# A decoder trunk with power-of-two weight scales: the cross-partition maxima of 20 of 22 scales are turned through DRAM instead of by TensorE

## The chip, the cores and the metric

The program runs on one core of one Trainium2 chip. The metric is the device time of one execution in microseconds (us); the kernel before takes 1691.45 us (median of three runs, 1690.5 to 1695.71). Engines are named as in the profile: PE (TensorE matmul), PEld (its weight load), DVE (VectorE), ACT (ScalarE), POOL (GpSimd), SP (SyncE, which here only issues DMAs).

## What is computed

A residual stream x of 2048 tokens by 1024 goes through one recurrent layer (layer A) and one attention layer (layer B), all in float32. Layer B reads keys and values that are projected once from layer A's output.

```python
def rglru_layer(x, ...):                       # layer A
    u = rmsnorm(x, norm_g) @ w_in              # 1024 -> 2 * 1536
    xb, gate = u[..., :LRU_WIDTH], u[..., LRU_WIDTH:]
    xb = causal_depthwise_conv(xb, conv_w, conv_b)
    r = sigmoid(blockdiag(xb, wr) + br); i = sigmoid(blockdiag(xb, wi) + bi)
    a = exp(-8 * r * softplus(-lam)); b = sqrt(1 - a * a) * (i * xb)
    hs = scan(h[t] = a[t] * h[t - 1] + b[t])
    return x + (hs * silu(gate)) @ w_out
# layer B: rmsnorm, q/gate projection, sliding-window attention
# with sinks and ALiBi, gate, output projection, residual
```

## The kernel before

**Two-part numbers.** Matmuls take f16 operands. Each float32 operand is scaled by a power of two and split into a high and a low f16 part (`split_flat`: ACT makes the high part, DVE the low one), and a product takes three passes. The scale of a weight matrix or of an activation comes from its largest magnitude. DVE finds a maximum per partition; `floor2` (line 95) then makes of `[128, n]` such maxima the largest of each column over all partitions, rounded down to a power of two, on every partition. That is the function that the change replaces.

**floor2 before** takes six steps on two engines. PE transposes the column into PSUM (`f2t`, line 100); DVE reduces the row to one number (`f2m`, 102), bounds it below (`f2n`, 104), masks the mantissa away (`f2o`, 106) and scales a small identity by it (`f2d`, 108); PE multiplies that by ones, which puts the number on all partitions (`f2b`, 110, two passes of the array); DVE copies it out of PSUM (111). Both PE steps stand in PE's queue between products that have nothing to do with them.

**Stages.** (1) The start loads and normalizes the first 512 tokens and the first weights. (2) Layer A runs 16 units: 4 groups `g` of three 128-channel tiles by 4 chunks `c` of 512 tokens. A unit (`unit`, line 370) is 72 products `pu` (x-branch), 72 products `pg` (gate branch) and 36 products `pr` (the two recurrence gates, `gate`, line 407). ACT copies `pu` out of PSUM into `u`; DVE convolves it to `xc`; ACT and POOL (DVE for one of three tiles) split `xc` into `hl`, which `pr` reads; SP copies a third of a block between partitions (`b3<-hl`, line 395), which the last 9 products of each gate read. The PSUM tiles of `pu`, `pg` and `pr` take turns in six banks, so the second gate's tiles wait until DVE has read the `pg` tiles (`gs<-pg`, line 404). Then ACT makes r, i, a and the square root, and DVE runs `ri`, `q`, the scan `h`, and the running maximum `ymx`. (3) The output projection of layer A: 16 token blocks of 72 products `po` (`out_block`, line 591), with `xnT<-xnT,sy` as the split of a block's input, two blocks ahead. (4) Layer B.

**Work beside a unit** comes from generators (`run_side`). While group g runs, the weights of group g + 1 are prepared: `prep_part` (263) loads two halves into `st`, reduces them (`amx`, `mx`, `m`), calls `floor2`, and splits into `w`; `prep_gates` (287) does the same for the gate weights `gst`. In group 0 the side work is the second weight half of group 0 and the normalization of the next chunk (`norm_chunk`, 248), whose result is turned by a DMA transpose (`flip`, 210: `xnT<-xs`). In group 3 it is the scale and split of `w_out` (`w_out_scale`, `w_out_prep`), and `y_scale` (541) turns `ymx` of a chunk into `sy`. Beside stage 3, `prep_rows` and `w_outB_scale` (665) make the weights of layer B.

**What sets the order.** Every engine runs its own queue strictly in order. A list scheduler fills the queues from priorities and its own estimates of durations; `floor2` is issued 200 places ahead (`tc.high_priority(offset=F2AHEAD)`). SP's queue holds all loads, the `b3` copies and the transposes, one after the other: a DMA whose condition is not met holds up all that stand behind it on SP.

**Calls of floor2:** the first weight half of group 0 and `conv_bounds` (both in the start), and 20 more: the other weight halves (`pw`, 4 + 3), the gate weights (`pwg`, 4), `w_out` (`pwo`), four chunks of y (`py`), and four weight sets of layer B (`pw_kv`, `pw_q`, `pw_g`, `pw_o`).

Of the kernel before, what the change touches and what calls it, by code (L numbers as in the profile page):

```python
# [12 lines left out]
F32 = mybir.dt.float32  # L13
# [3 lines left out]
U32 = mybir.dt.uint32  # L17
# [19 lines left out]
PREP_AT = (((1, 0), (3, 1), (7, 2), (9, 3)), ((1, 4), (3, 5), (5, 6), (7, 7)), ())  # L37
# other products woven in (columns / 2.4) after a block's pair of scores, before the first
# and the second half of its values; for the first block, the second, those between, the
# last but one, the last  # L40
GAPS = ((700, 8000, 9500), (300, 8000, 10500), (700, 8000, 9500), (800, 8000, 12000), (900, 11000, 9500))
# [12 lines left out]
def trunk(ctx, tc, x, wA, gw, par, gains, woA, wkv, wB, woB, vec, alib, out):  # L54
# [12 lines left out]

    # ---------------------------------------------------------------- constants
    id16 = xp.tile([P, P], F16, name="id16")
# [18 lines left out]

    cnt = [0]

    def uniq(s):
        cnt[0] += 1
        return f"{s}_{cnt[0]}"

    def floor2(mx, n, keep):
        """[P, n] maxima -> keep [P, n]: each column's maximum over the partitions, rounded
        down to a power of two, on every partition"""
        with tc.high_priority(offset=F2AHEAD):
            tp = pst([n, P], F32, "tp", uniq("f2t"), 2)
            pe.transpose(tp, mx, id32)  # L100
            m1 = xp.tile([n, 1], F32, tag="f2m", name=uniq("f2m"), bufs=2)
            dve.tensor_reduce(m1, tp, AX.X, ALU.max)
            m2 = xp.tile([n, 1], F32, tag="f2n", name=uniq("f2n"), bufs=2)
            dve.tensor_scalar(m2, m1, 1e-30, None, ALU.max)
            m3 = xp.tile([n, 1], F32, tag="f2o", name=uniq("f2o"), bufs=2)
            dve.tensor_scalar(m3.bitcast(U32), m2.bitcast(U32), 0x7F800000, None, ALU.bitwise_and)
            dg = xp.tile([n, n], F32, tag="f2d", name=uniq("f2d"), bufs=2)
            dve.tensor_scalar(dg, id32[:n, :n], m3, None, ALU.mult)
            bp = pst([P, n], F32, "tp", uniq("f2b"), 2)
            pe.matmul(bp, ones[:n, :], dg, start=True, stop=True)  # L110
            dve.tensor_copy(keep, bp)

    def col(name, n=1):
        return tmp[0].tile([P, n], F32, tag=f"{name}{n}", name=uniq(name), bufs=2)
# [3 lines left out]

    # ------------------------------------------------ conv and decay parameters
    cb2 = xp.tile([P, 2], F32, name="cb2")  # L120
# [13 lines left out]
    def decay():  # L134
        # softplus(-lam) = max(-lam, 0) + log1p(exp(-|lam|)), log1p(e) = 2 atanh(e / (2 + e))
        nlam = xp.tile([P, KR], F32, name="nlam")
# [25 lines left out]

    # ------------------------------------------------------------ shared pieces
    def wtile(name):
        return wp.tile([P, 2, 3072], F16, tag="W", name=name, bufs=4)

    def absmax_rows(src, nk, gcol, dest):
        """largest |gain * w| per partition of src [P, nk, n] -> dest [P, 1]"""
        a = col("amx", nk)
        dve.tensor_reduce(a, src, AX.X, ALU.max, apply_absolute_value=True)  # L170
        dve.tensor_tensor(a, a, gabs[:, gcol : gcol + nk], ALU.mult)
        dve.tensor_reduce(dest, a, AX.X, ALU.max)
# [6 lines left out]
    def split_flat(src, scale, hi, lo):  # L179
        """hi + lo = src * scale in two f16 parts"""  # L180
        act.activation(hi, src, AF.Copy, scale=scale)
        dve.scalar_tensor_tensor(lo, src, scale, hi, ALU.mult, ALU.subtract)  # L182

    def rstd10(ss, eng):
        """2**10 / rms of rows of D from their sums of squares"""
        var = col("var")
        eng.tensor_scalar(var, ss, 1.0 / D, EPS, ALU.mult, ALU.add)
        rs = col("rs")
        pool.tensor_tensor(rs, var, mhalf[:, 0:1], ALU.pow)
        r10 = col("r10")  # L190
        eng.tensor_scalar(r10, rs, 1024.0, None, ALU.mult)
        return r10

    def normalize(xb, hi, lo, rs=pool):
        """hi + lo = rows of xb [P tok, D] over their rms, times 2**10"""
        ss = col("ss")
        act.activation(lo.bitcast(BF16), xb, AF.Square, accum_out=ss)
        split_flat(xb, rstd10(ss, rs), hi, lo)
# [11 lines left out]
    def flip(src, dest):  # L210
        """dest[:, i, :] = the transpose of src[:, i * P : (i + 1) * P], two-byte types"""
        nc.sync.dma_start_transpose(dest, src)
# [12 lines left out]

    # ======================================================= layer A, channel-major
    p1pool = ExitStack()
# [16 lines left out]
    def xparts():  # L244
        """two [P, D] f16 tiles"""
        return tuple(p1.tile([P, D], F16, tag=f"ri{w}", name=uniq("xri"), bufs=4) for w in range(2))
# [60 lines left out]
    def scales_x(g, W):  # L307
        # |conv(u) + b| <= sum|w| * 2**11 px + max|b|
        px = W["p0"]
# [42 lines left out]
    def proj_first(w):  # L352
        """the first chunk's three tiles, token block by token block"""
        o = [pst([P, CH], F32, "mm", uniq("pu"), 6) for _ in range(3)]
# [15 lines left out]
    def unit(g, c, W):  # L370
# [36 lines left out]
        def gate(w):  # L407
            gt = W["gt"]
            o = [pst([P, CH], F32, "mm", uniq("pr"), 6) for _ in range(3)]
            for j in range(3):  # L410
                for n, (wi, xi) in enumerate(PASSES):
                    mm(o[j], gt[:, wi, w, j * P : (j + 1) * P], hls[j][:, xi], n == 0, False)
            # the fourth block, gathered, on the array's columns 0, 32 and 64
            for n, (wi, xi) in enumerate(PASSES):
# [60 lines left out]

    # ---- the first weights and tokens
    W0 = {}
# [26 lines left out]
    conv_bounds()  # L504
    scales_x(0, W0)

    def first_side():
# [72 lines left out]

    # ============================================================== out-proj of A
    bw = ctx.enter_context(tc.tile_pool(name="bw", bufs=1, side="right", reuse_waits="tile"))
# [39 lines left out]
    def bstage(n):  # L622
        """[P, n] f32 staging, n <= 2048"""
        stg[0] += 1
# [64 lines left out]
    for b in range(NB):  # L689
# [4 lines left out]
        if b == NB - 3:  # L694
            drain(side)
            # the first block of layer B
            fx = xnT[3].bitcast(F32)[:, 0:D]
# [5 lines left out]

    # ======================================================= layer B, token-major
    psA.close()
# [19 lines left out]

    # keys carry g_q * g_k / 8, scaled by a power of two
    gg = p3.tile([P, HD], F32, name="gg")
# [9 lines left out]
    dve.tensor_scalar(gk, gg, igg, 2048.0, ALU.mult, ALU.mult)  # L737
    # slopes halve from head h to head h + 2: queries of head h carry 2**(4 + h // 2), and
    # two tables do for all heads
    qsc = p3.tile([P, HEADS], F32, name="qsc")  # L740
# [16 lines left out]
    def eps_of(key, name):  # L757
        # eps in the units of the projection: eps * (2**24 / p)**2
        i = p3.tile([P, 1], F32, name=name + "i")
# [10 lines left out]
    dve.tensor_scalar(gscB, pB["g"], 2.0**-24, None, ALU.mult)  # L770
    # out = P * p_y * (p_wo * p_kv * 2**-31): y carries 2**3 / p_kv, its parts 2**14 / p_y, w_out 2**14 / p_wo
    cB = p3.tile([P, 1], F32, name="cB")
# [3 lines left out]
    def proj3(o, xt, w, n0, n1, nk=KD):  # L776
        """o[tok, n0:n1] = x @ w in three passes; yields their length after every few products"""
        i = 0
# [22 lines left out]
    def project(b):  # L801
# [3 lines left out]
        yield from proj3(kv, xt, kvrow, 0, 256)  # L805
        # ---- keys
        kn = p3.tile([P, 2, HD], F32, tag="kn", name=uniq("kn"), bufs=1)
# [22 lines left out]
        d["kT"] = kt  # L830
        # ---- values: |v| * 2**24 / p < 2**35, kept times 2**-21
        v32 = p3.tile([P, 2, HD], F32, tag="v32", name=uniq("v32"), bufs=2)
# [11 lines left out]
        d["v32"], d["vt"] = v32, vt  # L844
        # ---- queries
        qn = p3.tile([P, HEADS, HD], F32, tag="f4", name=uniq("qn"), bufs=2)
# [40 lines left out]
    def attend(b):  # L887
        """yields how much else the PE is to do, as in GAPS"""
        gaps = GAPS[b if b < 2 else max(2, b - NB + 5)]
# [39 lines left out]
        def turn(n, ph):  # L929
            flip(ph.rearrange("p w h n -> p (w h n)"), pT.rearrange("p w h n -> p (w h) n"))  # L930
            for w in range(2):
                # slot j > query q belongs to the block before
                pool.affine_select(  # L933
# [59 lines left out]
    def gated(b, y, i, parts):  # L993
        """part i of y times the gate, in two f16 parts, transposed"""
        d = st[b]
# [34 lines left out]
    def hooked(gen, hooks):  # L1030
        """gen with f run before its i-th item for the pairs i, f of hooks"""
        for i, t in enumerate(gen):
# [5 lines left out]
    def between(b):  # L1038
        """what the PE does beside block b's attention"""
        if b + 3 < NB:  # L1040
# [21 lines left out]
    def weave(main, fill):  # L1062
        """runs main; while it waits, takes as much from fill"""
        debt = 0.0
# [27 lines left out]
def _layout(inputs):  # L1092
# [3 lines left out]
    for g in range(NTRI):  # L1096
        for i, w in enumerate((wr, wi)):
# [5 lines left out]
            o[0:96, 384:480] = b[3]  # L1103
    # channels: tile j of a triple has block j and a third of block 3
    perm = []
# [54 lines left out]
```

## Time and profile before

| | us |
|---|---|
| median of three runs (lowest, highest) | 1691.45 (1690.5, 1695.71) |
| span of the profiled execution | 1695.6 |
| PE busy, share of the span | 1550.7 (91%) |
| DVE busy | 1198.8 (71%) |
| ACT busy | 742.7 (44%) |
| POOL busy | 475.5 (28%) |

The profiled execution's own time is its span, 1695.6 us; what lies around the span is not listed apart, and the slowest of the three runs, 1695.71, is 0.1 above it. A row of the timeline gives start, length, engine, line, operation, tile written <- tiles read, count, and in brackets the idle time of the engine just before, with what ended it. "PEclk" is the share of full clock that was granted to TensorE. A row of the groups gives count, busy time and mean length in ns, then the idle time just before such instructions with what ended it.

### The profile page before, as it was taken

The page shows a single profiled execution, that of the slowest core. Times are in us where ns is not written, and L with a number is a line of the kernel's source. Part 1 is how long each engine was busy: PE and PEld are TensorE (multiplying, and loading weights), DVE is VectorE, ACT ScalarE, POOL GpSimd, SP SyncE. Part 2 cuts the span into 40 slices and gives each one's busy share as a digit, 9 for nine tenths or more (in the row PEclk, how much of TensorE's full clock was granted, in tenths as well). Part 3 has the DMA queues.
Part 4 walks back from the last instruction along what each step waited for, and adds up shares of the span by engine and source line. Part 5 has one row for each costly group of instructions (what it writes and reads, how often), then busy time and mean ns, then how long its engine had stood idle before and what let it go on. Part 6 is the DMA issues. An engine that isn't in the chain of part 4 may idle for free.

```text
span 1695.6 us, 23216 instructions
## 1 busy us (share of the span) xinstructions
PE 1550.7 (91%) x8602; PEld 765.2 (45%) x8602; DVE 1198.8 (71%) x2700; ACT 742.7 (44%) x1229; POOL 475.5 (28%) x578
## 2 busy tenths in 40 slices
PE   5988889999999998999799978899999999999986
PEld 4433334444444443444344434455555555555543
DVE  6768878688766677766521269777777777777775
ACT  5656546555445465422200154434444434444332
POOL 2234222211222323000000233524343334334331
PEclk9999999999999999999899989999999999999999
DMA  6563212014311133677731334353344444444322
GB/s 206 142 135 92 79 54 80 24 54 127 106 36 32 57 109 112 220 246 260 283 98 62 117 92 91 78 103 84 85 91 91 91 91 90 88 91 90 66 63 66
DMA packets 242194, 177.29 MB, mean 105 GB/s; under 512 B 204704, under 2 KB 215200, under 8 KB 242080
## 3 DMA queue, kind: packets, MB, share of 16 engines
q1 hardware_dynamic: 233632, 146.95, 33.7%
q0 software_dynamic: 8304, 28.84, 5.0%
q8 instruction: 67, 1.10, 0.3%
q14 instruction: 47, 0.39, 0.1%
q10 hardware_dynamic: 144, 0.01, 0.0%
HBM read 92.93 MB, written 29.36 MB: 72 GB/s over the span
## 4 chain that ended last, share of the span: by engine, by line
PE 35%; DVE 24%; DMA 13%; issue 13%; POOL 7%; ACT 7%; SPq 0%; POOLq 0%; ACTq 0%; DVEq 0%
PE po L117 9%; PE pg L117 9%; PE pu L117 7%; PE pf L117 5%; DMA ppx<-ph 5%; DVE s L906 3%; PE pr L117 3%; DVE s L967 2%; DVE xc L390 2%; POOL hl L393 2%; DVE s L962 2%; DMA x<-x1D 1%; DVE h L448 1%; POOL ppx L933 1%; DMA st<-in_wA_dram 1%
## 5 line engine op out<-in xcount | busy, mean ns | idle before, releaser
L117 PEld LDWEIGHTS <-w 128*128 128x128 f16 x2520 | 238.8, 100 | 274.5 <-issue 22.2
L117 PE MATMUL pu<-xnT,w 128*128 128x512 f16 (+1 forms) x1368 | 262.2, 353 | 3.9 <-ACT ri L423 3.4
L117 PEld LDWEIGHTS <-xT 128*128 128x128 f16 x1920 | 186.9, 98 | 169.8 <-issue 3.8
L117 PE MATMUL pg<-xnT,w 128*128 128x512 f16 x1152 | 259.2, 386 | 0.2 <-DVE w L182 0.2
L117 PE MATMUL po<-wo,xnT 128*128 128x512 f16 x1152 | 252.7, 382 | 1.2 <-ACT ri L423 1.2
L117 PE MATMUL pf<-wob,yT 128*128 128x512 f16 x768 | 186.0, 395 | 3.0 <-DMA yT<-wob 1.9
L117 PE MATMUL pq<-wq,xT 128*128 128x512 f16 x768 | 175.9, 379 | 2.6 <-DVE gs L884 2.6
L117 PEld LDWEIGHTS <-xnT 128*128 128x128 f16 x1152 | 113.0, 98 | 137.5 <-issue 4.9
L117 PE MATMUL pg<-wq,xT 128*128 128x512 f16 x768 | 174.3, 381 | 0.0
L117 PEld LDWEIGHTS <-yT 128*128 128x128 f16 x768 | 74.7, 101 | 88.0 <-issue 7.1
L117 PE MATMUL po<-vt,ppx 128*128 128x128 f16 (+1 forms) x1024 | 65.8, 222 | 49.0 <-DMA ppx<-ph 33.6
L390 DVE SCALAR_TENSOR_TENSOR xc<-u,cwS,xc 128x512 f32<-128x512 f32 x144 | 109.5, 783 | 0.1
L933 POOL TENSOR_SCALAR_AFFINE_SELECT ppx<-ppx 128x1024 f16<-128x1024 f16 x64 | 79.0, 1256 | 65.7 <-DMA ppx<-ph 65.7
L117 PEld LDWEIGHTS <-ppx 128*128 128x128 f16 x1024 | 57.1, 107 | 79.6 <-DMA ppx<-ph 42.1
L385 POOL COPY uhist<-u 128x3 f32<-128x3 f32 x36 | 22.8, 633 | 235.9 <-ACT u L379 235.8
L117 PE MATMUL s<-kT,qT 128*128 128x256 f16 x512 | 75.2, 275 | 12.8 <-DVE s L962 11.7
L950 DVE TENSOR_TENSOR y<-y,po 128x256 f32<-128x256 f32 x64 | 26.7, 417 | 84.9 <-ACT y L949 84.6
L617 DVE SCALAR_TENSOR_TENSOR xnT<-po,cA,xnT 128x512 f32<-128x512 f32 x32 | 23.8, 747 | 88.4 <-PE po L117 88.4
L423 ACT ACTIVATE ri<-pr,pr,rsc 128x512 f32<-128x512 f32 x96 | 67.5, 776 | 42.4 <-PE pr L117 42.3
L906 DVE TENSOR_SCALAR s<-s,ssc,bi 128x128 f32<-128x128 f32 x256 | 84.4, 400 | 0.6
L393 POOL TENSOR_TENSOR hl<-xc,hl 128x512 f16<-128x512 f32 x32 | 58.7, 1842 | 83.9 <-ACT hl L392 83.8
L392 ACT CAST hl<-xc 128x512 f16<-128x512 f32 x48 | 29.6, 617 | 120.1 <-DVE xc L390 113.4
(239 smaller groups left out, 2358.3 us busy)
## 6 DMA issues: line engine op xcount, KB each, us to landing
xnT<-in_wB_dram SPq DMA_DIRECT2D x16, 1024.0 KB, 6.8
yD<-gs POOLq DMA_DIRECT2D x48, 256.0 KB, 2.8
wst<-in_woA_dram SPq DMA_DIRECT2D x24, 512.0 KB, 4.7
xnT<-yD SPq DMA_DIRECT2D x16, 768.0 KB, 6.3
st<-in_wA_dram SPq DMA_DIRECT2D x15, 768.0 KB, 5.4
xs<-in_x_dram SPq DMA_DIRECT2D x16, 512.0 KB, 5.0
xnT<-in_x_dram SPq DMA_DIRECT2D x16, 512.0 KB, 4.4
x1D<-xnT POOLq DMA_DIRECT2D x16, 512.0 KB, 3.3
```

The source lines that it names most:

```text
L117: pe.matmul(o, lhsT, rhs, start=start, stop=stop, skip_group_check=True)
L385: pool.tensor_copy(uhist[:, t], u[:, CH : CH + 3])
L390: dve.scalar_tensor_tensor(xc, u[:, d : d + CH], cw[:, j, d : d + 1], xc, ALU.mult, ALU.add)
L392: act.copy(hl[:, 0], xc)
L393: (pool if j in LO_POOL else dve).tensor_tensor(hl[:, 1], xc, hl[:, 0], ALU.subtract)
L423: act.activation(v, o[j], AF.Sigmoid, bias=pr[:, t, 5 + w : 6 + w], scale=W["rsc"])
L617: dve.scalar_tensor_tensor(xs_, o[n], cA[c], xs_, ALU.mult, ALU.add)
L906: dve.tensor_scalar(s[:, h], s[:, h], ssc[:, h : h + 1], bi[:, h : h + 1], ALU.mult, ALU.add)
L933: pool.affine_select(pU[:, w], pT[:, w], [[0, 8], [-1, P]], ALU.is_gt, 0.0, base=0, channel_multiplier=1)
L950: dve.tensor_tensor(yv, yv, o[:, :, 0], ALU.add)
L962: dve.copy_predicated(sl, mask.unsqueeze(1).to_broadcast([P, 2, P]), o[:, :, 0:P])
L967: dve.tensor_tensor_reduce(s[:, h], s[:, h], al[:, i * P : (i + 1) * P], 1.0, -3.4e38, ALU.add, ALU.max, mr[:, h : h + 1])
```

## The change

After the start, `floor2` no longer uses PE. The `[128, n]` maxima are written to a DRAM tile `f2r` as rows of 128 numbers (one DMA that writes 4 bytes from each partition); a second DMA reads that row back to all 128 partitions (`f2w`, 512 bytes into each); DVE reduces it (`f2m`), bounds it and masks it, straight into the result. Both DMAs are issued by SP, the second after the first has landed. The first two calls stay as they were.

```diff
+    started = [False]
-    def floor2(mx, n, keep):
+    def floor2_pe(mx, n, keep):
         with tc.high_priority(offset=F2AHEAD):
             tp = pst([n, P], F32, "tp", uniq("f2t"), 2)
             pe.transpose(tp, mx, id32)
...
             pe.matmul(bp, ones[:n, :], dg, start=True, stop=True)
             dve.tensor_copy(keep, bp)
+    def floor2(mx, n, keep):
+        if not started[0]:
+            floor2_pe(mx, n, keep)
+            return
+        with tc.high_priority(offset=F2AHEAD):
+            turned = dr.tile([n, P], F32, name=uniq("f2r"))
+            nc.sync.dma_start(turned.rearrange("n p -> p n"), mx)
+            row = xp.tile([P, n, P], F32, tag="f2w", name=uniq("f2w"), bufs=2)
+            nc.sync.dma_start(row, turned.unsqueeze(0).to_broadcast([P, n, P]))
+            m1 = xp.tile([P, n], F32, tag="f2m1", name=uniq("f2m1"), bufs=2)
+            dve.tensor_reduce(m1, row, AX.X, ALU.max)
+            m2 = xp.tile([P, n], F32, tag="f2m2", name=uniq("f2m2"), bufs=2)
+            dve.tensor_scalar(m2, m1, 1e-30, None, ALU.max)
+            dve.tensor_scalar(keep.bitcast(U32), m2.bitcast(U32), 0x7F800000, None, ALU.bitwise_and)
...
     conv_bounds()
     scales_x(0, W0)
+    started[0] = True
```

The scheduler lays out the queues anew. On PE, the 20 pairs of `f2t` and `f2b` are gone and the products follow each other in the same order. On PE in the output projection, where block 9 begins (`xnT_99` is block 8's input, `xnT_97` that of block 9), the queue before reads:

```order
L117 MATMUL po_6942<-wo_6061,xnT_99 128x512
L117 LDWEIGHTS xnT_97
L117 MATMUL po_7045<-wo_5134,xnT_97 128x512
L100 MATMUL f2t_7004<-id_74,m_7002 1x128
L117 LDWEIGHTS xnT_97
L117 MATMUL po_7045<-wo_5134,xnT_97 128x512
```

`f2t_7004` waits there for `m_7002`, the maximum of layer B's output weights; in the changed queue block 9's products stand without it.

On DVE at the turn from group 0 to group 1 (`m_2099` and, changed, `m_1958` and `m_2083` are the partition maxima of weights; `ri` is work of the unit that ends), before:

```order
L293 TENSOR_REDUCE m_2099<-gst_2097 128x1
L102 TENSOR_REDUCE f2m_1975<-f2t_1973 1x1
L104 TENSOR_SCALAR f2n_1977<-f2m_1975 1x1
L106 TENSOR_SCALAR f2o_1979<-f2n_1977 1x1
L108 TENSOR_SCALAR f2d_1981<-id_74,f2o_1979 1x1
L111 COPY pw_300_1972<-f2b_1983 128x1
L102 TENSOR_REDUCE f2m_2104<-f2t_2102 1x1
```

and changed:

```order
L292 TENSOR_REDUCE m_1958<-mx_1921 128x1
L311 TENSOR_REDUCE m_2083<-gst_2081 128x1
L461 SCALAR_TENSOR_TENSOR ri_1641<-xc_1376,isig_333,ri_1641 128x512
L461 SCALAR_TENSOR_TENSOR ri_1643<-xc_1426,isig_333,ri_1643 128x512
L461 SCALAR_TENSOR_TENSOR ri_1645<-xc_1476,isig_333,ri_1645 128x512
L126 TENSOR_REDUCE f2m_297_1965<-f2w_1963 128x1
L128 TENSOR_SCALAR f2m_298_1967<-f2m_297_1965 128x1
L129 TENSOR_SCALAR pw_294_1960<-f2m_298_1967 128x1
```

The three `ri` now stand between the maxima and the reduction that needs them back from DRAM.

On SP at the end of the first unit (group 0, chunk 0; `st` are weight loads, `b_65` is that unit's `b3`, `xnT_98` the transposes for chunk 1), before:

```order
L261 DMA st_1733<-in_wA_dram 128x4x384
L261 DMA st_1901<-in_wA_dram 128x4x384
L395 DMA b_65_349<-hl_705 32x1024
L239 DMA xs_104<-in_x_dram 128x1024
L395 DMA b_65_349<-hl_650 32x1024
L395 DMA b_65_349<-hl_800 32x1024
L212 DMA_TRANSPOSE xnT_98<-xs_103 128x16x128
L212 DMA_TRANSPOSE xnT_98<-xs_104 128x16x128
```

and changed:

```order
L413 DMA b_65_349<-hl_701 32x1024
L413 DMA b_65_349<-hl_650 32x1024
L413 DMA b_65_349<-hl_792 32x1024
L279 DMA st_1725<-in_wA_dram 128x4x384
L257 DMA xs_104<-in_x_dram 128x1024
L279 DMA st_1889<-in_wA_dram 128x4x384
L122 DMA f2r_1777<-m_1774 128x1
L124 DMA f2w_1779<-f2r_1777 128x128
L230 DMA_TRANSPOSE xnT_98<-xs_103 128x16x128
L230 DMA_TRANSPOSE xnT_98<-xs_104 128x16x128
```

The two weight loads moved behind the `b3` copies, and a pair of the new DMAs stands ahead of the two transposes. Layer B's queues are unchanged.

## The prediction

> **What bounds the kernel now.** I read the share of busy time by stage first (start, layer A, output projection, layer B: PE, PEld, DVE, ACT, POOL busy, granted clock, DMA share, GB/s), with one stretch inside layer A apart.
>
> ```profile
> 0.00:60.00 60.00, 39.63 (x412) 32.09 (x413) 45.13 (x112) 33.42 (x50) 14.02 (x35) 0.94 0.61 199
> 60.00:690.00 630.00, 587.55 (x2808) 254.51 (x2807) 478.76 (x796) 353.81 (x510) 173.31 (x218) 0.97 0.29 84
> 690.00:910.00 220.00, 209.14 (x960) 94.25 (x959) 115.58 (x160) 52.79 (x54) 10.32 (x19) 0.98 0.60 204
> 450.00:590.00 140.00, 140.00 (x689) 61.60 (x684) 93.19 (x136) 73.59 (x105) 34.49 (x48) 1.00 0.15 46
> ```
>
> PE is the bound of both stages that the change touches: in 450 to 590, where no scale is taken, it is busy all 140 us. So PE's idle time is what can be won, and the groups say how much of it stands before the two steps of `floor2`.
>
> ```profile
> L110 PE MATMUL f2b<-f2d,ones 1*128 1x1 f32 (+1 forms) x44 | 9.0, 272 | 17.0 <-DVE f2d L108 16.8 <-DVE m L274 0.2
> L100 PE MATMUL f2t<-id,m 128*1 128x128 f32 x21 | 6.3, 301 | 36.3 <-DVE m L274 19.8 <-DVE m L676 9.0 <-DVE m L543 5.7
> 12.58 0.37 PE L100 MATMUL f2t<-id,m 128*1 128x128 f32 x1 [12.58 <-DVE m L274]
> 16.14 0.58 PE L110 MATMUL f2b<-f2d,ones 1*128 1x1 f32 x2 [3.18 <-DVE f2d L108]
> 32.52 0.38 PE L110 MATMUL f2b<-f2d,ones 2*128 2x2 f32 x2 [0.22 <-DVE m L274]
> ```
>
> Of 36.3 + 17.0 = 53.3 us, the last three rows (12.58 + 3.18 + 0.22 = 16.0) belong to the two calls that stay. **37.3 us of PE's waiting goes with the 20 pairs.** PE stood still because its queue is in order and DVE, which makes `m` and `f2d`, was late.
>
> **What goes, beside the waits.** The largest stall shows the rest:
>
> ```profile
> 841.87 0.37 PE L100 MATMUL f2t<-id,m 128*1 128x128 f32 x1 [8.96 <-DVE m L676]
> 842.04 5.71 PE L117 MATMUL po<-wo,xnT 128*128 128x512 f16 x14
> 847.68 0.38 PE L110 MATMUL f2b<-f2d,ones 1*128 1x1 f32 x2
> 847.99 67.30 PE L117 MATMUL po<-wo,xnT 128*128 128x512 f16 x311
> 842.00:847.70 5.70, 5.70 (x16) 0.55 0.80 283
> 249.90:253.40 3.50, 3.50 (x10) 0.53 0.00 0
> 357.90:361.00 3.10, 3.10 (x11) 0.68 0.09 21
> 594.60:597.40 2.80, 2.80 (x8) 0.50 0.04 8
> ```
>
> A pair holds PE for 0.17 us (841.87 to 842.04) and 0.31 us (847.68 to 847.99): 0.48, times 20 = 9.6. And after a stall PE runs at a lower granted clock (last four rows, clock ahead of the DMA share): 14 products take 5.71 us where 311 take 67.3, 0.216 each. The stretches lose 5.7 x 0.45 = 2.6, 3.5 x 0.47 = 1.6, 3.1 x 0.32 = 1.0 and 2.8 x 0.50 = 1.4, together 6.6. The whole price on PE is 37.3 + 9.6 + 6.6 = 53.5 us; no more can be won.
>
> The Trainium skill, "TensorE: Matmul & The Clock Gate", Part 1, says that the clock halves after about 3.4 us of idleness. The trace disagrees: the wait ahead of 594.6 was 2.26 us (row below) and the clock fell to 0.50. By the page, the losses at 357.9 and 594.6 would not be stalls' work, and the sum below would be 2.4 us smaller.
>
> **What comes.** No row shows the two new DMAs. The nearest are the partition copies `b3` and, with 128 short rows like these, the parameter load behind the start's loads:
>
> ```profile
> b<-hl SPq DMA_DIRECT2D x48, 64.0 KB, 1.9
> pr<-in_par_dram SPq DMA_DIRECT2D x1, 48.0 KB, 9.1
> L395 SPq DMA_DIRECT2D b<-hl x48: 507/512/614, 58.1 to 678.6; - x48
> 170.56 0.27 DVE L102 TENSOR_REDUCE f2m<-f2t 1x1 f32<-1x128 f32 x1
> 174.02 1.28 DVE L444 SCALAR_TENSOR_TENSOR q<-ri,q 128x512 f32<-128x512 f32 x2
> ```
>
> A round trip is two issues and two landings: 2 x (0.5 + 1.9) = 4.8 us, between 3.8 (issue inside the landing) and 2 x 0.5 + 9.1 + 1.9 = 12.0. I take 4.8, since layer A loads little: 84 GB/s on the mean in the second row of the first fence. DVE's own work shrinks a little: five short steps become three, and the reduction still reads 128 elements (0.27, third row). But `f2m` now holds DVE's queue until the trip ends, and what stands behind it is the unit's own work: `q`, the scan, the next unit's `xc`, and through these `hl` on POOL and `pr` on PE. At the turn to group 1 DVE spent 174.02 - 170.56 = 3.5 us on two calls (last two rows), from the first `f2m` to `q`, waits for `f2b` included. In the changed queue three `ri` stand between, work that is done either way; the pair of trips, one behind the other on SP, then ends some 5.5 us after the first maximum, of which the second maximum and the `ri` cover 3. The rest and six short steps come to about 3.5 again. I count DVE as even, and at the other calls too.
>
> **Which stalls are on the path.** A PE stall gained is kept only if PE isn't stopped next by DVE. Place by place:
>
> *Start to 206: 0.* The weight loads go behind the `b3` copies on SP.
>
> ```profile
> 45.00 1.64 SPq L261 DMA_DIRECT2D st<-in_wA_dram  x2
> 59.41 1.15 SPq L395 DMA_DIRECT2D b<-hl  x2
> 67.89 4.98 SPq L212 DMA_TRANSPOSE xnT<-xs  x2
> 74.77 5.52 PE L117 MATMUL pu<-xnT,w 128*128 128x512 f16 x17 [3.38 <-ACT ri L423]
> 110.62 0.81 PE L117 MATMUL pr<-hl,gw 128*128 128x512 f16 x3 [1.57 <-POOL hl L393]
> 112.71 0.59 PE L117 MATMUL pr<-hl,gw 128*128 128x512 f16 x2 [1.28 <-POOL hl L393]
> 114.75 1.47 PE L117 MATMUL pr<-b,gw 96*32 96x512 f16 x9 [1.45 <-DMA b<-hl]
> 149.21 0.38 PE L110 MATMUL f2b<-f2d,ones 1*128 1x1 f32 x2 [2.16 <-DVE f2d L108]
> ```
>
> They start at about 60.6 (59.41 + 1.15) instead of 45. With a 512 KB load between them that is 2.05 MB, at the start's 199 GB/s 10.3 us: 71. DVE's reduction of the second (1.75, row below) stands ahead of the last `gs` (0.74) and the two normalizations that the transposes wait for, and these took 4.98: 71 + 1.75 + 0.74 + 4.98, and as much again for normalizing and landing as before, puts chunk 1's first product at about 82 where it stood at 74.77, 7 us late. PE then waits less at 110 to 115 (4.3) and not at 149 (2.16 + 0.48); that returns 6.9. Ends: -7 to +7.
>
> *Around 250: 3.7.* Here the stall covers another wait.
>
> ```profile
> 244.89 0.39 PE L117 MATMUL pr<-hl,gw 128*128 128x512 f16 x1
> 249.76 0.36 PE L100 MATMUL f2t<-id,m 128*1 128x128 f32 x1 [4.48 <-DVE m L274]
> 246.85 1.75 DVE L170 TENSOR_REDUCE amx<-st 128x4 f32<-128x1536 f32 x1 [4.57 <-DMA st<-in_wA_dram]
> 248.51 0.74 DVE L404 SCALAR_TENSOR_TENSOR gs<-pg,gsc,gs 128x512 f32<-128x512 f32 x1
> 254.44 4.92 PE L117 MATMUL pu<-xnT,w 128*128 128x512 f16 x22
> ```
>
> The second gate's third tile needs the bank that `gs` frees at 249.25, and `gs` stands behind `amx`, which waits for a load. Then come three products (0.65) and nine `b3` ones (0.83): 250.7 instead of 254.4.
>
> *357, 594, 637 and 674: 4.0 + 4.6 + 3.5.*
>
> ```profile
> 357.59 0.38 PE L110 MATMUL f2b<-f2d,ones 1*128 1x1 f32 x2 [2.57 <-DVE f2d L108]
> 594.19 0.38 PE L110 MATMUL f2b<-f2d,ones 1*128 1x1 f32 x2 [2.26 <-DVE f2d L108]
> 637.48 0.27 PE L100 MATMUL f2t<-id,m 128*1 128x128 f32 x1 [2.94 <-DVE m L543]
> 674.30 0.27 PE L100 MATMUL f2t<-id,m 128*1 128x128 f32 x1 [2.77 <-DVE m L543]
> 797.26 0.27 PE L100 MATMUL f2t<-id,m 128*1 128x128 f32 x1 [1.90 <-DVE m L635]
> ```
>
> The first two are free of neighbours: 2.57 + 0.48 + 1.0 and 2.26 + 2 pairs at 0.48 + 1.4. At 637 and 674 the scale of y is now awaited on DVE ahead of the last `gs`, whose bank PE needs: of 2.94 + 2.77 and 2 x 0.48 I keep half.
>
> *Output projection: 14.* Its products wait only for block splits, made two blocks ahead. 8.96 + 0.48 + 2.6 at 841, 1.90 + 0.48 at 797, three pairs at 0.48: 15.9, less 2 for `f2m` waits ahead of the splits.
>
> Against it, 2 us: the splits of `w_out` move into the dense stretch 450 to 590. The other pairs I leave at nothing: what PE gains there, DVE's chain takes.
>
> **Sum:** 0 + 3.7 + 4.0 + 4.6 + 3.5 + 14 - 2 = 27.8 us, made against the profiled 1695.6 (to 1667.8). The median of the runs stands 4.2 lower, so the forecast is 1691.45 - 27.8 = **1664 us**. Layer B keeps its queues.
>
> **Rivals.**
> - *DVE's chain takes all of layer A's gain* (chance 0.20): the loop of 250 (ACT, DVE, POOL, `b3`, load, `amx`, `gs`) sets every unit, and the late chunk 1 isn't returned. 14 - 7 = 7 won: 1684. For it: the 4.57 us wait of `amx`; against: PE alone fills 450 to 590.
> - *Nothing is left* (0.08): the new DMAs also hold SP's loads in the output projection, and half of its 14 goes: 7 - 7, 1691.
> - *The trip is long* (0.12), the side that is slower. Place: `f2m` at the head of DVE's queue at 12 points of layer A (of its 15 calls, three pairs wait together). Each us beyond 4.8 costs up to 12 us; 27.8 / 12 = 2.3, so it decides from a trip of 7.1 us. At 12.0, with half of it hidden, 12 x 7.2 / 2 = 43 goes: 1691.45 - 27.8 + 43 = 1707. For it: 9.1 us for 128 short rows; against: that load stood behind 768 KB loads.
> - *All of it comes* (0.12): 53.5 less 7 for the start: 1645.
>
> The Trainium skill, "DMA: Bandwidth & Descriptors", Rules for kernel authors, speaks for the long trip: a transpose by a plain DMA with a rearranged access pattern is 19 times slower than the hardware one, and a strided last dimension costs a descriptor per element. No run here shows it for 128 elements.
>
> **Chances and range.** The forecast has 0.48. Faster by over 0.3% (5 us, what a measurement here can tell from no change): 0.48 + 0.20 + 0.12 = 0.80; within: 0.08; slower: 0.12. The range 1645 to 1690 leaves out the slower case and most of "nothing left".
>
> **What would show it.** `f2m` on DVE waiting under 3 us on `f2w`, and landings near 2 us, bear the trip out; over 5 us, the long one. Chunk 1's first `pu` near 82 instead of 74.8 shows the moved loads. PE without a gap from 760 to 900 shows the output projection. I am wrong if `pr` waits for `b3`, `hl` or `gs` grow by what the pairs gave back.

## The result, and the profile after

The changed kernel takes **1783.65 us** (median of 4 runs, 1776.51 to 1788.68) beside 1692.55 for the kernel before: ratio 1.0548, 95% interval 1.0525 to 1.057. The forecast was 1664, within 1645 to 1690. The time lies outside the range, on the side to which the long trip had been given 0.12.

The page of the changed kernel: span, engines, shares of the chain of work that ended last, and the groups that answer to those of before (busy time, mean ns | idle time of the engine just before them, and what ended it).

```profile
span 1774.7 us, 23128 instructions
PE 1573.0 (89%) x8542; PEld 761.4 (43%) x8542; DVE 1193.1 (67%) x2660; ACT 740.6 (42%) x1229; POOL 472.5 (27%) x578
...
DVE 28%; DMA 21%; PE 20%; issue 17%; ACT 7%; POOL 7%; SPq 0%; POOLq 0%; ACTq 0%; DVEq 0%
...
L135 PE MATMUL pr<-hl,gw 128*128 128x512 f16 x288 | 90.9, 458 | 43.3 <-DVE gs L422 25.3
...
L126 DVE TENSOR_REDUCE f2m<-f2w 128x1 f32<-128x128 f32 x20 | 5.7, 284 | 151.1 <-DMA f2w<-f2r 151.1
```

On the chain of work that ended last PE had 35% before; now DVE has 28%, DMA 21% and PE 20%. DVE is no busier than before (1193.1 us against 1198.8), but it stands idle for 151.1 us at one group: the reduction `f2m` of the row that comes back from DRAM. In the stretch 60 to 690, which held 587.55 us of PE work before, PE is busy 555.67, at a lower granted clock (third number from the end).

```profile
60.00:690.00 630.00, 555.67 (x2531) 233.50 (x2530) 440.55 (x713) 324.64 (x474) 160.09 (x209) 0.92 0.28 77
```

One call on the chain of work that ended last (start, length, what):

```profile
325.39 0.17 DVE m L292
325.57 7.52 DMA f2r<-m
333.11 4.80 DMA f2w<-f2r
337.93 0.30 DVE f2m L126
```

The trip through DRAM takes 12.3 us: 7.52 to write 512 bytes, 4.80 to read them back. Over all 20 calls the list of DMA issues (KB, median us to landing) says 7.9 + 4.9 = 12.8:

```profile
f2w<-f2r SPq DMA_DIRECT2D x20, 64.0 KB, 4.9
f2r<-m SPq DMA_DIRECT2D x20, 0.5 KB, 7.9
```

What stands behind `f2m` is seen in the timeline of that place, ACT and DVE:

```profile
331.93 1.67 ACT L456 ACTIVATE q<-q 128x512 f32<-128x512 f32 x3
327.51 2.07 DVE L461 SCALAR_TENSOR_TENSOR ri<-xc,isig,ri 128x512 f32<-128x512 f32 x3
337.93 0.29 DVE L126 TENSOR_REDUCE f2m<-f2w 128x1 f32<-128x128 f32 x1 [8.35 <-DMA f2w<-f2r]
339.73 1.28 DVE L462 SCALAR_TENSOR_TENSOR q<-ri,q 128x512 f32<-128x512 f32 x2
```

ACT has all three `q` by 333.60. DVE finished `ri` at 329.58, then waits 8.35 us at `f2m`, runs the short steps of the scale and begins `q` at 339.73, 6.1 us after the data was there. The scan, the next `xc`, `hl` and PE's `pr` follow that much later.

**Where the time went, by stage.** PE's first `po` ends layer A, its first `pkv` ends the output projection. Layer A ends at 764.6 instead of 688.5 (+76.1), the output projection takes 266.2 instead of 265.0 (+1.2), layer B 743.9 instead of 742.1 (+1.8): together the 79.1 between the two spans. The medians lie 91 apart: the profiled execution of before was a long one, that of the change the shortest of its four. Layer B has the same queues in all kernels below, yet its length in their profiles goes from 737.5 to 749.2 us; why stays open, and differences of a few us between two profiles are read with that in mind.

PE feels it in the products `pr` of layer A, which wait for `gs` and for `b3`. The wait view (in all us, times, longest), two rows of before and one of the change, whose wait for `gs` is in the groups above (25.3):

```profile
PE pr L117 <- DVE gs L404: 5.9, 3, 3.7
PE pr L117 <- DMA b<-hl: 4.5, 4, 1.9
...
PE pr L135 <- DMA b<-hl: 30.7, 14, 7.7
```

### The profile page after: what moved, and what is told of

Read it like the earlier page. It is cut to its first block, busy times and chain, and to the rows that moved or that the text cites. A ratio compares the mean times of both kernels' runs of the same rounds, so it can differ in the third digit from the quotient of the medians.

```text
span 1774.7 us, 23128 instructions
## 1 busy us (share of the span) xinstructions
PE 1573.0 (89%) x8542; PEld 761.4 (43%) x8542; DVE 1193.1 (67%) x2660; ACT 740.6 (42%) x1229; POOL 472.5 (27%) x578
## 4 chain that ended last, share of the span: by engine, by line
DVE 28%; DMA 21%; PE 20%; issue 17%; ACT 7%; POOL 7%; SPq 0%; POOLq 0%; ACTq 0%; DVEq 0%
PE po L135 6%; PE pf L135 5%; DMA f2r<-m 5%; DMA ppx<-ph 4%; PE pg L135 3%; DVE xc L408 3%; DVE s L925 2%; DMA f2w<-f2r 2%; DVE s L986 2%; PE pu L135 2%; DVE h L466 2%; DVE s L981 2%; POOL hl L411 2%; DMA st<-in_wA_dram 2%; DMA x<-x1D 2%
## 5 line engine op out<-in xcount | busy, mean ns | idle before, releaser
L135 PE MATMUL pu<-xnT,w 128*128 128x512 f16 (+1 forms) x1368 | 265.0, 356 | 13.2 <-DMA xnT<-xs 9.9
L135 PE MATMUL pg<-xnT,w 128*128 128x512 f16 x1152 | 255.0, 382 | 14.1 <-ACT w L199 11.8
L135 PE MATMUL pr<-hl,gw 128*128 128x512 f16 x288 | 90.9, 458 | 43.3 <-DVE gs L422 25.3
L126 DVE TENSOR_REDUCE f2m<-f2w 128x1 f32<-128x128 f32 x20 | 5.7, 284 | 151.1 <-DMA f2w<-f2r 151.1
L135 PEld LDWEIGHTS <-gw 128*128 128x128 f16 (+1 forms) x576 | 39.0, 108 | 154.1 <-issue 119.1
```

The source lines that it names most:

```text
L135: pe.matmul(o, lhsT, rhs, start=start, stop=stop, skip_group_check=True)
```

## The experiments

The theory **T1**: DVE, in order, stands at `f2m` for a trip of 12.3 us, and its own work of the unit comes late. Rivals: **T2**, SP's queue is held by the second DMA until the first has landed (in the profile after, `f2w` waits for `f2r` 105.8 us in all), and the `b3` copies and loads behind it come late; **T3**, the DMAs take bandwidth from the others. The table has all timed kernels, in order of the wait at `f2m`; a stage's length is read from one profile. A ratio is to runs of the kernel before that were taken with that kernel (their medians: 1689.47 to 1692.55), so times of two rows compare to within some 3 us.

| kernel | median us | ratio to before (95%) | wait at f2m for f2w | layer A ends | output projection |
|---|---|---|---|---|---|
| before | 1692.55 | 1 | none | 688.5 | 265.0 |
| dve_in_outproj | 1679.89 | 0.9931 (0.9905, 0.9957) | none | 688.6 | 248.9 |
| dve_only | 1681.8 | 0.9944 (0.9922, 0.9965) | none | 687.2 | 251.2 |
| idle_trips | 1712.61 | 1.0111 (1.0074, 1.0148) | none (row unread) | 695.8 | 273.3 |
| short_trip | 1691.58 | 0.9999 (0.998, 1.0017) | 40.2 | 691.4 | 250.5 |
| outproj_only | 1699.01 | 1.0037 (1.0021, 1.0053) | 52.0 | 688.1 | 269.8 |
| wide_pieces | 1697.11 | 1.0054 (1.0031, 1.0077) | 57.0 | 694.9 | 252.3 |
| pinned_later | 1759.4 | 1.0397 (1.0373, 1.042) | 113.0 | 745.4 | 268.4 |
| pieces_128 | 1771.88 | 1.0472 (1.0446, 1.0499) | 134.7 | 757.5 | 263.3 |
| from_group_1 | 1760.54 | 1.0393 (1.0361, 1.0425) | 139.7 | 746.0 | 267.6 |
| take_later | 1773.54 | 1.0485 (1.0446, 1.0523) | 147.3 | 762.6 | 263.0 |
| the change | 1783.65 | 1.0548 (1.0525, 1.057) | 151.1 | 764.6 | 266.2 |
| pieces_64 | 1786.1 | 1.0551 (1.052, 1.0582) | 151.7 | 768.1 | 270.2 |
| double_trip | 1882.4 | 1.1126 (1.109, 1.1161) | 238.7 | 833.8 | 306.1 |

### DVE or SP: idle_trips

```diff
     def floor2(mx, n, keep):
...
+        floor2_pe(mx, n, keep)
         with tc.high_priority(offset=F2AHEAD):
             turned = dr.tile([n, P], F32, name=uniq("f2r"))
...
-            dve.tensor_reduce(m1, row, AX.X, ALU.max)
```

> PE makes the scale as in the kernel before, and SP sends the same pair of DMAs for each of the 20 calls, whose row nobody reads. T1 (DVE stands at f2m until the trip ends): without that wait the time is that of before, 1692, within 8. T2 (SP's queue, held by the second DMA until the first lands, delays the b3 copies and loads behind it): most of the loss stays, 1750 or more. T3 (traffic): as T2, but with the b3 landings longer than 1.9 us.

PE, DVE, ACT and POOL have the same queues as before the change, and SP waits at the second DMA about as long as in the changed kernel, 99.0 us beside 105.8 (the wait view of SP's queue: in all, times, longest):

```profile
SPq L125 <- DMA f2r<-m: 99.0, 17, 8.9
```

Yet the loss is 1.1% (0.74 to 1.48), 13 to 25 us, instead of 5.5%. **T1 carries most of the loss; SP's hold or the traffic carries a smaller share**, in both stages (+7.3, +8.3). The forecast of T1, within 8 us of before, was too low by that share. The sign that was named for T3 is absent: a `b3` copy lands after 1.9 us, as before. T2 and T3 weren't parted further.

### No trip at all: dve_only, dve_in_outproj

```diff
+            tq = xp.tile([P, 32], F32, tag="f2t", name=uniq("f2t"), bufs=2)
+            dve.transpose(tq, mx.to_broadcast([P, 32]))
+            dve.tensor_reduce(m1, tq, AX.X, ALU.max)
+            for i in range(4):
+                dve.tensor_copy(m4[:, i : i + 1], m1[32 * i : 32 * i + 32])
+            dve.tensor_reduce(m2, m4, AX.X, ALU.max)
+            dve.tensor_scalar(m2, m2, 1e-30, None, ALU.max)
+            for i in range(4):
+                dve.tensor_scalar(keep[32 * i : 32 * i + 32].bitcast(U32), m2.bitcast(U32), 0x7F800000, None, ALU.bitwise_and)
```

> No PE and no DMA in the 20 calls: DVE transposes 32 by 32 blocks of the repeated maxima, reduces, brings the four quarters together and masks (12 short steps where before there were six on DVE and two on PE). T1: with no trip to wait for, the prediction's terms without its long trip stand: PE loses the pairs and their waits, 1691.45 - 27.8 = 1664, and up to 20 x 8 more short steps at about 0.1 us come on top if DVE is in the way: 1664 to 1680. If PE's waits were only cover for DVE's chain (the prediction's first rival), 1684 to 1691.

> PE makes the 15 scales of layer A as before; in the five calls beside the output projection DVE does the work alone, as in dve_only. That stage took 251.2 us in dve_only and 265.0 before, layer A 687.2 and 688.5. If the whole gain lies in the output projection, as these profiles say and as the prediction had it for that stage (14): 1692 - 14 = 1678, within 4. If layer A's pairs were worth more by the median than by one profile: 1682 or more.

Both beat both kernels: 0.6% and 0.7% faster than before. PE's timeline of dve_only at the call around 250, and in the output projection:

```profile
248.28 1.08 PE L135 MATMUL pr<-hl,gw 128*128 128x512 f16 x3 [3.14 <-DVE gs L422]
249.29 1.47 PE L135 MATMUL pr<-b,gw 96*32 96x512 f16 x9
250.69 9.48 PE L135 MATMUL pu<-xnT,w 128*128 128x512 f16 x40
...
687.19 251.37 PE L135 MATMUL po<-wo,xnT 128*128 128x512 f16 x1152 [3.24 <-ACT ri L441]
```

The 1152 products of the output projection run without a gap: the stage's 14 us are real. Layer A ends 1.3 us earlier only. dve_only fell just outside its 1664 to 1680, 2 us below the 1684 of the first rival; dve_in_outproj, which leaves layer A to PE, is as fast within the intervals. The gain lies in the output projection.

### The trip there alone: outproj_only, and the start: from_group_1

```diff
     scales_x(0, W0)
-    started[0] = True
...
     y_scale(NCH - 2)
+    started[0] = True
     drain(w_out_prep(3))
```

That is outproj_only; in from_group_1 the line stands in `first_side`, behind group 0's own two calls.

> Only the five calls beside the output projection (the last chunk of y but one, and the four weight sets of layer B) go through DRAM; the 15 others stay on PE. T1 at 12.3 us a trip: the output projection took 265.0 before and 266.2 with the change, so 1693 within 5. The prediction's step for that stage (14 won), if only layer A spoils it: 1678. T2 puts the loss on SP's queue, which holds the loads of this stage too: 1700 or more.

> The two calls of group 0's own weights (the second half and the gates) stay on PE, 18 go through DRAM. By the first product of chunk 1, which came 16.9 us later with the change: 1783.65 - 17 = 1767, within 5, if what was lost at the start stays lost. If later waits swallow it: 1775 to 1784.

The five calls are those of the last chunk of y (not the last but one, as the expectation has it) and of layer B's four weight sets. With the trip they make that stage 269.8 us, where DVE alone takes 248.9 (dve_in_outproj). DVE stands at `f2m`, the split of a block's input comes late, and PE waits for it. PE of outproj_only, the longest waits:

```profile
820.89 1.03 PE L135 MATMUL po<-wo,xnT 128*128 128x512 f16 x2 [7.86 <-ACT xnT L199]
879.13 78.89 PE L135 MATMUL po<-wo,xnT 128*128 128x512 f16 x358 [2.90 <-DVE xnT L200]
```

Its 1699 is a little above T1's 1693 within 5; T2's "1700 or more" can't be excluded by this run alone. In from_group_1, whose start has no trip, 23 us come back (18.6 in layer A) where 17 were expected: what the start lost had stayed lost.

### Longer and shorter trips: double_trip, short_trip

double_trip adds a second trip, of column 0 of the row, before DVE reduces both; in short_trip DVE first makes the maximum of each 32 partitions:

```diff
+            nc.sync.dma_start(again.rearrange("n p -> p n"), row[:, :, 0])
+            nc.sync.dma_start(row[:, :, P : 2 * P], again.unsqueeze(0).to_broadcast([P, n, P]))
             m1 = xp.tile([P, n], F32, tag="f2m1", name=uniq("f2m1"), bufs=2)
```

```diff
+            dve.transpose(tq, mx.to_broadcast([P, 32]))
+            dve.tensor_reduce(m4, tq, AX.X, ALU.max)
+            turned = dr.tile([4, 1], F32, name=uniq("f2r"))
+            nc.sync.dma_start(turned, m4[0:P:32])
-            nc.sync.dma_start(turned.rearrange("n p -> p n"), mx)
```

> The number makes the trip through DRAM twice, one after the other, before DVE reduces both rows: 24.6 us instead of 12.3. T1, 8.3 us per us of trip from no trip to one: 1886, and more where a second trip finds less cover (up to 16 per us, all 20 calls by 0.8: 1980). If the loss is not the length of the trip but something that each call costs once (a missed slot on SP, a clock drop): 1784 to 1800.

> DVE first reduces each quarter of 32 partitions (a 32 by 32 transpose of the repeated maxima and a reduction), and only 4 numbers go through DRAM and back: no row of 128 pieces. First leg near 1.4 us (as 4 bytes per partition into rows 512 bytes apart), second 2 to 2.8 (as a row written in one piece and read by all), so a trip near 4.8, the one the prediction took. The prediction's sum, with its trip but its other steps untested: 1664 (1645 to 1690). T1 with no free cover in layer A: DVE alone gave 1681.8 with no trip and the change 1783.65 with 12.3 us, 8.3 us per us of trip; at 4 to 5 us that makes 1715 to 1723.

double_trip came out at 1882.4 where 1886 was said; its `f2m` waits 238.7 us. short_trip gave about the trip that the prediction had taken. Its chain of work has the second call of a pair:

```profile
252.06 2.48 DMA f2r<-f2q
254.55 2.88 DMA f2w<-f2r
```

That call took 5.4 us (2.48 + 2.88). A single call of layer A is shorter: SP issues the write at 293.90 and the read at 295.46, 1.6 us later, and the read lands after 2.5 (median), 4.1 together; in the output projection it is longer. With trips of 4.1 to 5.4 us the time is that of before, 1691.58: not the prediction's 1664, and better than T1's straight line (1715 to 1723). In its profile the output projection ends 11.6 us earlier than before (941.9 against 953.5), and layer B then takes 747.5 us where it took 742.1. A trip of that length is covered in part: `f2m` waits in 11 of 20 calls, 40.2 us in all. The output projection took 250.5 us, PE's work in one piece again, though `f2m` waits there too (23.2 us of the 40.2): the splits two blocks ahead cover it. Layer A ended at 691.4, 3 us later than before.

### Only the length of the trip: pieces_64, pieces_128

As short_trip with almost the same queues, but more of the quarter maxima make the trip (here 64; for pieces_128 all):

```diff
-            turned = dr.tile([4, 1], F32, name=uniq("f2r"))
-            nc.sync.dma_start(turned, m4[0:P:32])
+            turned = dr.tile([64, 1], F32, name=uniq("f2r"))
+            nc.sync.dma_start(turned, m4[0:P:2])
```

> As short_trip, with the engines' queues all but the same, but 64 of the 128 quarter maxima are written to the row (each quarter sixteen times) and the row of 256 bytes is read back. If the pieces written into one row make the trip long, the first leg lies between 1.6 us (4 pieces) and 7.4 (128): 0.047 us a piece, 4.4 us at 64, and the second between 2.7 and 4.7: 3.7; trip 8.1. T1: on the line from short_trip (about 4.5 us, 1691.6) to the change (12.3 us, 1783.65), 11.8 per us: 1734, within 10. If what counts is only whether DVE has to wait at all: no more than 1710.

> As short_trip with the same queues, but all 128 quarter maxima are written and the row of 512 bytes is read back: the trip of the change, 12.3 us, with nothing else altered against short_trip. T1: the change's time plus the two short DVE steps, 1784 to 1795. If the change's new order of instructions made the loss, and not the trip: near short_trip's 1691.6.

DMA issues (KB, median us to landing) of pieces_64:

```profile
f2w<-f2r SPq DMA_DIRECT2D x20, 32.0 KB, 4.7
f2r<-f2q SPq DMA_DIRECT2D x20, 0.2 KB, 8.1
```

and of pieces_128:

```profile
f2w<-f2r SPq DMA_DIRECT2D x20, 64.0 KB, 4.6
f2r<-f2q SPq DMA_DIRECT2D x20, 0.5 KB, 7.2
```

The trip alone, 4.1 to 5.4 against 11.8 us (7.2 + 4.6), makes 80 us between short_trip and pieces_128: it is the length of the trip, and not the new order of instructions. SP's queue is held longer too, but by idle_trips that is the smaller share. But 64 pieces took as long as 128; my price per piece was wrong, and with it that kernel's expected time. By its trip of 12.8 us the 1786.1 fits.

### Later consumers: take_later, pinned_later

```diff
-        floor2(m, 1, pw)
+        row = send(m, 1)
+        for _ in range(4):
+            yield 1
+        take(row, 1, pw)
```

> The 14 calls of weight scales from group 1 on are parted: the maxima are sent off where they were, and the reduction of the row, with all that hangs on it, is issued four steps of the side work later (some 11 us in layer A); the y scales and group 0's calls are as in the changed kernel. T1 (DVE stands at the head of its queue): the wait at f2m falls from 151 us to under 80 and the time to 1710 to 1740. T2 (SP stands): the second DMA still holds SP as long, 1760 or more. If the late weights themselves were what PE waits for: no better than 1784.

> As take_later, whose wait at the reduction stayed at 147 us in 16 places, with the reductions this time held behind everything that was issued on DVE before them, so that in layer A seven of them stand 30 to 110 DVE steps behind the maxima. T1: at those calls the wait at f2m goes and with it up to 7/20 of the loss: 1740 to 1760. If late weights cost what DVE's standing cost: 1775 or more.

take_later missed: it says nothing on T1, since DVE's queue came out almost as in the change and the wait stayed. The scheduler, it seems, put `f2m` where it reckoned that the row landed, whatever the place in the program. pinned_later, two steps later instead of four, adds the order that was missing:

```diff
-            dve.tensor_reduce(m1, row, AX.X, ALU.max)
+            tc.keep_in_program_order(dve.tensor_reduce(m1, row, AX.X, ALU.max))
```

The wait view (in all us, times, longest) of take_later:

```profile
DVE f2m L134 <- DMA f2w<-f2r: 147.3, 16, 15.7
```

and of pinned_later:

```profile
DVE f2m L134 <- DMA f2w<-f2r: 113.0, 12, 15.2
```

34 us less of the wait, 14 us less of time (layer A 17 us shorter); what took back the rest of the wait was not tried apart. So part of the trip can be hidden by placing its consumer late, though far from all of it.

### What makes the trip long: legs, legs_size, wide_pieces

```python
d = dr.tile([1, P], F32, name=f"wcol{k}{r}")                          # legs
q.dma_start(d.rearrange("n p -> p n"), step(f"g{k}{r}")[:, 0:1])
back(f"rrow{k}{r}", d.to_broadcast([P, P]), q)
q.dma_start(d, step(f"a{n}x{r}")[0 : P : P // n, 0:1])                 # legs_size, n pieces
q.dma_start(d[:, 0:1], step(f"b{m}x{r}")[:, 0:1])                      # legs_size, m * 4 bytes apart
```

> A program of its own that leaves out the whole computation and writes zeros: single small DMAs, each after the one before has landed, four of each kind, nothing else loading. T1 (the trip is long by itself): the column of 4 bytes per partition into one DRAM row takes about 7.4 us from issue to landing and the row back to all partitions about 4.8, as in the changed kernel's chain of waits. T3 (the trip is long through other traffic there): both near 2 us, as a b3 copy. What makes the first leg long is told by the variants: if the 128 writes into one 512-byte row are the cause, the same 4 bytes into rows 512 bytes apart take about 2 us; if small elements are, those take 7 us as well and whole rows of 512 bytes take 2; if it is the queue, ScalarE's or GpSimd's queue differs from SP's.

SP's timeline of legs, the first column and the read behind it, and the DMA issues (`wcol`: 4 bytes of each partition into one row; `rrow`: that row to all; `rone`: a row written in one piece to all; `wgap`: 4 bytes of each partition 512 bytes apart; S, A, P: SP's, ScalarE's, GpSimd's queue):

```profile
3.02 0.32 SPq L80 DMA_DIRECT2D wcolS<-gS  x1
10.32 0.32 SPq L73 DMA_DIRECT2D rrowS<-wcolS  x1
...
rrowS<-wcolS SPq DMA_DIRECT2D x4, 64.0 KB, 4.6
rone<-wone SPq DMA_DIRECT2D x4, 64.0 KB, 2.8
wcolA<-gA ACTq DMA_DIRECT2D x4, 0.5 KB, 7.3
wcolP<-gP POOLq DMA_DIRECT2D x4, 0.5 KB, 7.4
wgap<-i SPq DMA_DIRECT2D x4, 0.5 KB, 1.4
```

The leg is as long with nothing else loading, 7.3 us (3.02 to 10.32): T3 is not what makes the trip long, nor is SP's queue. The same 512 bytes take 1.4 us when the pieces lie apart.

> A program of its own that leaves out the whole computation and writes zeros: single DMAs one after the other, three of each kind: n pieces of 4 bytes (4, 8, 16, 32, 64, 128 partitions) side by side in one DRAM row and that row back to all partitions; then 128 pieces 8, 16, 32, 64, 128 and 256 bytes apart. A price per piece (my estimate before pieces_64, 0.047 us) would give a straight line from 1.6 us at 4 pieces to 7.4 at 128; pieces_64 with 8.1 speaks against it. If pieces that share a stretch of DRAM wait for each other, the time depends on how many share it: it rises with n up to the size of the stretch and stays there, and with 128 pieces it falls with the distance, to about 1.4 us where each has a stretch of its own. If the number of pieces alone counts, distance changes nothing until 512 bytes.

SP's timeline of legs_size; the issue of the read (`rn`, `rm`) shows when the write before it had landed (the first of three rounds):

```profile
12.67 0.53 SPq L81 DMA_DIRECT2D wn16x<-a16x  x1
14.37 0.32 SPq L73 DMA_DIRECT2D rn16x<-wn16x  x1
18.54 0.49 SPq L81 DMA_DIRECT2D wn32x<-a32x  x1
21.81 0.32 SPq L73 DMA_DIRECT2D rn32x<-wn32x  x1
27.08 0.47 SPq L81 DMA_DIRECT2D wn64x<-a64x  x1
34.48 0.32 SPq L73 DMA_DIRECT2D rn64x<-wn64x  x1
39.81 0.32 SPq L81 DMA_DIRECT2D wn128x<-a128x  x1
46.55 0.32 SPq L73 DMA_DIRECT2D rn128x<-wn128x  x1
51.44 0.32 SPq L86 DMA_DIRECT2D wm2x<-b2x  x1
54.44 0.32 SPq L73 DMA_DIRECT2D rm2x<-wm2x  x1
57.30 0.32 SPq L86 DMA_DIRECT2D wm4x<-b4x  x1
58.75 0.32 SPq L73 DMA_DIRECT2D rm4x<-wm4x  x1
```

Side by side, 16 pieces take 1.7 us, 32 take 3.3, 64 take 7.4, 128 take 6.7. 128 pieces 8 bytes apart take 3.0, 16 bytes apart 1.45. So neither the number of pieces nor their size alone is the price, but many small pieces in the same stretch of DRAM. In the other rounds 64 took 8.1 and 8.0 and 128 took 6.6 and 7.1; why 64 take longer stays open.

```diff
+            dve.tensor_copy(four, mx.to_broadcast([P, 4]))
+            turned = dr.tile([P, 4], F32, name=uniq("f2r"))
+            nc.sync.dma_start(turned, four)
-            nc.sync.dma_start(turned.rearrange("n p -> p n"), mx)
```

> The change with one difference: DVE repeats each maximum four times and the first DMA writes 16 bytes from each partition instead of 4; the row that comes back is 2 KB. If the 4-byte pieces side by side make the first leg long, as legs_size has it (6.7 us side by side, 1.4 from 16 bytes apart on), the leg falls from 7.4 to about 1.5 us in the kernel too. The second leg of 2 KB has no row; between the 4.9 us of the 512-byte row and twice that. T1: trip 6.4 to 11; on the line from short_trip (4.1 us, 1691.6) to pieces_128 (11.8, 1771.9), 10.4 per us: 1716 to 1763. If the first leg is as long as before: 1784 or more.

The DMA issues of wide_pieces:

```profile
f2w<-f2r SPq DMA_DIRECT2D x20, 256.0 KB, 4.5
f2r<-f2q SPq DMA_DIRECT2D x20, 2.0 KB, 2.4
```

Sixteen bytes from each partition instead of four, four times the data, and the first leg falls from 7.9 to 2.4 us (medians, two calls together included), the time from 1783.65 to 1697.11. **The 4-byte pieces that lie side by side cost the change 84 to 87 of its 91 us** (87 by the medians, 84 by the ratios, 5.5% against 0.5%). The time is below the 1716 to 1763 that the straight line gave: short trips are covered in part.

## Why the prediction was wrong

**The step that failed** is "*I take 4.8, since layer A loads little*", and with it "*I count DVE as even, and at the other calls too*". The trip was 12.3 to 12.8 us, just above the upper end of the prediction's own bounds, 12.0. The nearest row was chosen by its bytes and by the traffic beside it (`b3`, 64 KB in 1.9 us); what counts is how the bytes lie. Roughly, by the medians: of the 120 us between 1664 and 1783.65, 92 are the length of the trip (from short_trip to the change); 18 are in terms that have no trip (from 1664 to dve_only, 1681.8). The 10 between dve_only and short_trip (1691.58) can't be put down to its trips alone: DVE is not even, it waits 40.2 us at `f2m`, but in the two profiles the output projection ends only 3.5 us later (938.4 and 941.9), and the rest lies in layer B.

The Trainium skill, "DMA: Bandwidth & Descriptors", Rules for kernel authors, which the prediction named for the long trip, pointed the right way. Its price, a descriptor per element, is not what the runs show, since 128 elements 16 bytes apart take 1.45 us.

**The long trip as a rival** had the right mechanism and end, and too small a price. It put 1707 on a trip of 12.0: twelve points of layer A, half hidden. It left out the output projection, which took 266.2 us where dve_only needed 251.2. DVE waits at 16 of the 20 reductions, and beyond a wait of some 57 us nearly all of it reaches the end: from wide_pieces to double_trip the wait grows by 181.7 us (238.7 - 57.0) and the time by 185.3 (1882.4 - 1697.11). Below that it costs little: 57.0 us of wait and 15 us of time between dve_only and wide_pieces, 52.0 and 19 between dve_in_outproj and outproj_only. By the medians, trips of 4.1 to 5.4 us already leave no gain (short_trip, as before), where the rival had 7.1: there was less to gain than 27.8, and layer B's spread is part of it.

**The other steps**, by dve_only, which has neither trip nor PE pair. Its 12 short DVE steps are part of what it shows, and single profiles differ by a few us. The stretches below add up to 15 us, the medians to 9 (1681.8 against 1690.78). The first product of a unit, or of the output projection, in the profile before and in dve_only, and from it what each stretch gave:

| stretch, ends at (before, dve_only) | forecast | measured |
|---|---|---|
| start to the fifth unit's `pu` (208.79, 208.50) | 0 | +0.3 |
| to the call around 250 (254.44, 250.69) | 3.7 | +3.5 |
| 357 and what follows (453.08, 452.32) | 4.0 | -3.0 |
| splits of `w_out` in the dense stretch (563.16, 570.00) | -2 | -7.6 |
| 594, 637, 674 (688.54, 687.19) | 4.6 + 3.5 | +8.2 |
| output projection (265.0, 251.2 long) | 14 | +13.8 |

Four of six stand. (Half of 2.94 + 2.77 + 0.96 at 637 and 674 is 3.3, where the prediction wrote 3.5.) The first product after the call around 250 was forecast for 250.7 and came at 250.69, for the reason given: PE waits 3.14 us for `gs`. Two terms of layer A were off. At 357 the gain went to DVE's chain: PE's wait for `f2d` was gone, and PE waited for `b3` (1.40 at 362.96) and `gs` (3.66, below) instead. The stretch without gaps, into which the splits of `w_out` moved, lost 7.6 instead of 2. short_trip's profile lost as much there (450.66 to 568.31), that of dve_in_outproj, where PE makes layer A's scales as before, nothing (453.88 to 563.96); that it is the splits was not tried apart. PE of dve_only in both:

```profile
368.85 1.44 PE L135 MATMUL pr<-hl,gw 128*128 128x512 f16 x3 [3.66 <-DVE gs L422]
...
524.50 0.86 PE L135 MATMUL pr<-b,gw 96*32 96x512 f16 x9 [1.46 <-DMA b<-hl]
...
531.56 17.39 PE L135 MATMUL pu<-xnT,w 128*128 128x512 f16 x72 [1.79 <-ACT ri L441]
```

So even a trip of no length would not have brought the forecast: 1681.8, not 1664. That lies near the first rival's 1684, which had layer A giving nothing (so it is, 1.3 us by the profiles) and the start losing 7 (it did not, +0.3): in part luck.

**The start** did lose with the trip: the first `pu` of chunk 1 stood at 74.77, was forecast for 82 and came at 91.65, behind the normalized input:

```profile
91.65 3.64 PE L135 MATMUL pu<-xnT,w 128*128 128x512 f16 x9 [9.91 <-DMA xnT<-xs]
```

dve_only, without a trip, had it at 77.70. The other 14 us are the long trips; those of group 0's own two calls cost 23 us to the end (from_group_1).

**What the prediction said would show it** did: 14 of the 16 waits at `f2m` are longer than 7 us, where over 5 was to mean the long trip; the waits of `pr` for `gs` and `b3` grew from 5.9 and 4.5 to 25.3 and 30.7 us.

## What to carry to other kernels

On an engine that works its queue in order, a wait for a transfer can cost nearly its whole length once it exceeds what the engine can do without (here 185 us of time for 182 us of wait); ask for the transfer's length first, and place its consumer late by an explicit order if the scheduler reckons it shorter. The Trainium skill, "DMA: Bandwidth & Descriptors", Rules for kernel authors, has the second half as: issue the DMA early and wait late; pinned_later agrees, 14 us below take_later. A column of single numbers is better not written side by side to DRAM: repeat each to 16 bytes, or reduce it on DVE, which was the fastest way here, at 5 calls as at 20.

## What the runs showed of the hardware

- 512 bytes to DRAM took 6.7 us as 128 pieces of 4 bytes side by side, 3.0 at 8 bytes apart, 1.45 at 16 bytes apart, and 1.1 from one partition in one piece (in legs, from issue to the next issue: 40.95 to 42.04).
- Read back by all 128 partitions, a 512-byte row took 4.6 us where it had been written in pieces just before and 2.8 where it had been written in one (legs); why was not tried. A row of 2 KB, written in pieces of 16 bytes, took no longer (4.5, wide_pieces).
- ScalarE's and GpSimd's queues are no faster for it: 7.3 and 7.4 us.
